# RWKV-7 time mixing by a timetable: two pairs of heads side by side, keys projected ahead

## The chip, the cores and the metric

The kernel runs on one core of one Trainium2 chip. The metric is the device time of one execution in microseconds (us), the median of several runs. The core's engines run side by side, each taking its own instructions in a fixed order: TensorE (PE, with its weight loads shown as PEld), VectorE (DVE), ScalarE (ACT), GpSimd (POOL) and SyncE (SP), which issues nearly all transfers from HBM. Engines wait for one another through semaphores. [...]

## The reference

Two layers over 256 tokens of width 2048. Layer A is RWKV-7 time mixing and a squared-ReLU MLP, layer B chunked attention on shared keys and values and another such MLP. Each sub-layer has an RMS norm in front with shift and scale from `c`, and a gate behind. The change is in the time mixing:

```python
xr, xw, xk, xv, xa, xg = [h + xx * mu[j] for j in range(6)]
r = xr @ w_r;  k = xk @ w_k;  v = xv @ w_v
w_log = -jax.nn.softplus(-(w0 + jnp.tanh(xw @ w1) @ w2)) - 0.5
a = jax.nn.sigmoid(a0 + (xa @ a1) @ a2)
g = jax.nn.sigmoid(xg @ g1) @ g2
kk = heads(k * k_k);  kk = kk / max(|kk|, 1e-12);  k = k * (1 + (a - 1) * k_a)
def step(S, inp):                      # one token, per head
    sa = einsum('bhvk,bhk->bhv', S, -kk_t)
    S = S * w_t + sa (kk_t * a_t) + v_t k_t
    y = einsum('bhvk,bhk->bhv', S, r_t)
y = group_norm(y) * ln_w + ln_b + sum(r * k * r_k) * v
return (y * g) @ w_o
```

There are 32 heads of 64. Instead of 256 steps the kernel takes four chunks of 64 tokens, with a triangular matrix inverted per chunk and head.

## The kernel before, in words

Activations lie with features on the 128 partitions and the 256 tokens along the row, so two heads, called a pair, fill the partitions, and there are 16 pairs. Every large product is done in two halves: a weight block of 128x1024 f32 is loaded into a `raw` tile (`raw`, line 350; 6 tiles), ACT casts it to the rounded half `wH` (L360), DVE makes the rest `wL` (L363), and per 128 input features `proj2` (L394, L395) issues one 512-column matmul with `wH` and one 256-column matmul with `wL`. Such a couple is called a dense unit below: a whole 2048-wide output block of 128 features is 16 units.

The program's stages in time: the norm, the token-shifted mixtures and the values (0 to 221 us); time mixing (221 to 764 us); the output projection `out_proj`; the MLP of layer A in four quarters, each with 16 up and 16 down blocks; shared keys and values, attention, its output projection; the second MLP.

Time mixing is written as generators per pair (`class Pair`): a projection of `k` and `r` (`proj_steps`, 32 dense units), `early` (decay, gates, normalisation: ACT and DVE on 128x256 tiles), `invert` (the triangular inverse by five doubling levels, each of them PE, ACT, PE, DVE; line 103 is the 32x32 matmul) and `late` (four chunks one after the other, each of three short dependent steps, then the group norm). In each period of 16 slots one pair is in each of the four stages, so a pair takes four periods and there are 19 periods; in the last three the first products of `out_proj` (`out_steps`) take the place of the dense part. The order on each engine is set by the tile framework's planner when the program is built, with `tc.issue_after` holding dense units and small steps of a slot in turn. Sums over a head (`head_sums`, L120) are two 256-column matmuls on the halves `sH` and `sL`, the second of which POOL makes (L115).

Beside all this runs `ada`: the shifts, scales and gates are 384 steps after the first stage, each a 128x1024 load into the same `raw` tiles and one DVE multiply-add into `acc` (L421, L423). `ada()` takes one step where the code calls it: 6 per period of time mixing, one per block of `out_proj`, four per three blocks of an MLP. `ada_need` runs all steps still missing for the parts that are named.

Of the kernel before, what the change touches and what calls it, by code (L numbers as in the profile page):

```python
# [32 lines left out]
        "w0", "a0", "k_k", "k_a", "r_k", "ln_w", "ln_b"]  # L33
# [3 lines left out]
def _constants():  # L37
# [23 lines left out]
    p = np.arange(P)  # L61
    bones = (p[:, None] // C == p[None, :] // C).astype(np.float32)
    put("bones", bones)
# [10 lines left out]
class Pair:  # L74
# [3 lines left out]
    EARLY = 8  # L78

    def __init__(self, body, j, v, tw, ta, tg, e01):  # L80
        self.b, self.j, self.v, self.tw, self.ta, self.tg, self.e01 = body, j, v, tw, ta, tg, e01
        self.heads = (slice(0, C), slice(C, P))

    def s(self, name="s", bufs=10):
        return self.b.pw.tile([P, T], F32, tag=name, bufs=bufs, name=name)

    def big(self, name, bufs):
        return self.b.pw.tile([P, 4, P], F32, tag=name, bufs=bufs, name=name)

    @staticmethod  # L90
    def ch(t):
        return t.rearrange("p (c t) -> p c t", t=C)

    def each(self, o, lhsT, rhs):
        for c in range(4):
            for K in self.heads:
                self.b.nc.tensor.matmul(o(c)[K], lhsT(c)[K], rhs(c)[K], start=True, stop=True)  # L97

    def tiles(self, o, lhsT, rhs, pairs):

        for c in range(4):
            for R, K in pairs:
                self.b.nc.tensor.matmul(o[QS[K], c, :], lhsT[QS[R], c, :], rhs[QS[R], c, :], start=True, stop=True,  # L103
                                        tile_position=(H * R, H * K))

    def parts(self, func, src, scale=1.0):

        nc, pw = self.b.nc, self.b.pw
        H, L = (pw.tile([P, T], F32R, tag=n, bufs=2, name=n) for n in ("sH", "sL"))
        nc.scalar.activation(H, src, func, scale=scale)  # L110
        if func != AF.Copy:
            t = self.s("pt", 2)
            nc.scalar.activation(t, src, func, scale=scale)
            src = t
        nc.gpsimd.tensor_tensor(out=L, in0=src, in1=H, op=ALU.subtract)  # L115
        return H, L

    def head_sums(self, ps, parts):
        for i, t in enumerate(parts):
            self.b.nc.tensor.matmul(ps, self.b.bones, t, start=(i == 0), stop=(i == 1))  # L120

    def early(self):
        b, nc, j, k, r, v, s, ch = self.b, self.b.nc, self.j, self.k, self.r, self.v, self.s, self.ch
        pw, vec, cst, e01 = b.pw, b.vec, b.cst, self.e01
        lw = pw.tile([96, 2, P], F32, tag="lw", bufs=2, name="lw")
        nc.sync.dma_start(out=lw, in_=b.d["lora2"][j, :96, 0:2])
        self.lg = pw.tile([P, 2, P], F32, tag="lg", bufs=2, name="lg")
        nc.sync.dma_start(out=self.lg, in_=b.d["lora2"][j, :, 2:4])
        z = b.psm()
        nc.tensor.matmul(z[:, 0:T], lw[:, 0, :], self.tw, start=True, stop=True)  # L130
        nc.tensor.matmul(z[:, T:2 * T], lw[:, 1, :], self.ta, start=True, stop=True)

        sw, a = s(), s()
        for o, at, b0 in ((sw, 0, "w0"), (a, T, "a0")):
            nc.vector.tensor_scalar(out=o, in0=z[:, at:at + T], scalar1=vec(b0, j), scalar2=-80.0,
                                    op0=ALU.add, op1=ALU.max)
            nc.scalar.activation(o, o, AF.Exp, scale=-1.0)
# [55 lines left out]
    def invert(self):  # L193
# [23 lines left out]
        for i, K in enumerate(QS):  # L217
            n = H * (i % 2)
            nc.scalar.copy(da[K], pg[K, :, n:n + H])
            if i % 2 == 0:  # L220
                nc.scalar.mul(co[K], pg[K, :, H:C], -1.0)
# [869 lines left out]
```

## Time and profile before

| what | us |
|---|---|
| median of 3 runs | 2779.97 |
| runs, lowest to highest | 2776.5 to 2784.27 |
| profiled execution | 2773.6 |
| its span, first to last instruction | 2771.8 |
| busy time of PE, of the span | 2653.9 (96%) |
| busy time of DVE | 2087.3 (75%) |
| busy time of ACT | 1260.9 (45%) |
| busy time of POOL | 301.8 (11%) |

Busy time of PE counts each matmul from its start to a modelled end; small matmuls overlap in it. So the distance from one start to the next says more on PE than the share. The transfers moved 662.60 MB, 239 GB/s on average. The stages differ much: time mixing has its transfers at half load, the first MLP at nine tenths.

### The profile page before, as it was taken

The page shows a single profiled execution, that of the slowest core. Times are in us where ns is not written, and L with a number is a line of the kernel's source. Part 1 is how long each engine was busy: PE and PEld are TensorE (multiplying, and loading weights), DVE is VectorE, ACT ScalarE, POOL GpSimd, SP SyncE. Part 2 cuts the span into 40 slices and gives each one's busy share as a digit, 9 for nine tenths or more (in the row PEclk, how much of TensorE's full clock was granted, in tenths as well). Part 3 has the DMA queues.
Part 4 walks back from the last instruction along what each step waited for, and adds up shares of the span by engine and source line. Part 5 has one row for each costly group of instructions (what it writes and reads, how often), then busy time and mean ns, then how long its engine had stood idle before and what let it go on. Part 6 is the DMA issues. An engine that isn't in the chain of part 4 may idle for free.

```text
span 2771.8 us, 57644 instructions
## 1 busy us (share of the span) xinstructions
PE 2653.9 (96%) x23402; PEld 2217.6 (80%) x23402; DVE 2087.3 (75%) x3098; ACT 1260.9 (45%) x2214; POOL 301.8 (11%) x416
## 2 busy tenths in 40 slices
PE   6998999999998999999999899999989999999997
PEld 3677777777887888888888788877878888888886
DVE  4568778878889888888788896799786566665665
ACT  2345555556344434344344354465444344443444
POOL 0003443443220000000000200000100000000002
PEclk9999999999999999999999999999999999999999
DMA  9886556555687888888888868888876555555553
GB/s 297 269 281 193 169 171 196 176 176 162 216 302 243 298 308 305 300 314 296 299 306 302 304 218 282 268 293 268 279 242 216 187 186 186 187 183 189 185 188 122
DMA packets 217387, 662.60 MB, mean 239 GB/s; under 512 B 21408, under 2 KB 68896, under 8 KB 217120
## 3 DMA queue, kind: packets, MB, share of 16 engines
q1 hardware_dynamic: 215056, 656.36, 71.5%
q8 instruction: 184, 3.01, 0.4%
q10 hardware_dynamic: 2064, 2.54, 0.3%
q14 instruction: 83, 0.68, 0.1%
HBM read 656.72 MB, written 2.10 MB: 238 GB/s over the span
## 4 chain that ended last, share of the span: by engine, by line
PE 76%; DVE 9%; DMA 7%; issue 4%; POOL 1%; ACT 1%; DVEq 0%; SPq 0%; ACTq 0%; POOLq 0%
PE pj L394 40%; PE pj L395 20%; DMA raw<-w_ada 5%; DVE wL L363 3%; DVE acc L423 2%; PE iv L103 2%; PE gr L97 1%; DMA raw<-w_ada_kv 1%; PE m L625 1%; DVE un L504 1%; PE o L383 1%; PE ms L97 1%; POOL sL L115 1%; PE chn L276 1%; DVE aHL L506 1%
## 5 line engine op out<-in xcount | busy, mean ns | idle before, releaser
L394 PE MATMUL pj<-aHL,wH 128*128 128x512 f32 x3712 | 1353.5, 405 | 26.0 <-DVE aHL L506 22.4
L360 ACT CAST wH<-raw 128x1024 fp32r<-128x1024 f32 x772 | 807.0, 1047 | 949.4 <-PE pj L394 622.1
L363 DVE TENSOR_TENSOR wL<-raw,wH 128x1024 fp32r<-128x1024 f32 x772 | 946.1, 1228 | 290.7 <-ACT wH L360 288.8
L395 PE MATMUL pj<-aHL,wL 128*128 128x256 f32 x3712 | 1049.3, 283 | 7.5 <-DVE wL L363 7.2
L394 PEld LDWEIGHTS pj<-aHL,wH 128*128 128x128 f32 x3712 | 700.3, 189 | 199.2 <-issue 28.0
L394 PE MATMUL pj<-hHL,wH 128*128 128x512 f32 x2048 | 722.0, 397 | 4.5 <-DVE hHL L882 4.5
L395 PEld LDWEIGHTS pj<-aHL,wL 128*128 128x128 f32 x3712 | 705.3, 190 | 14.6 <-DVE wL L363 11.9
L395 PE MATMUL pj<-hHL,wL 128*128 128x256 f32 x2048 | 574.3, 281 | 4.6 <-DVE wL L363 4.5
L423 DVE SCALAR_TENSOR_TENSOR acc<-raw,ct,acc 128x1024 f32<-128x1024 f32 x360 | 470.4, 1307 | 139.8 <-DMA raw<-w_ada 104.0
L394 PEld LDWEIGHTS pj<-hHL,wH 128*128 128x128 f32 x2048 | 384.3, 188 | 97.9 <-DVE hHL L882 6.7
L395 PEld LDWEIGHTS pj<-hHL,wL 128*128 128x128 f32 x2048 | 386.8, 189 | 8.1 <-DVE wL L363 7.7
L482 POOL TENSOR_TENSOR ss<-ss,sq 128x256 f32<-128x256 f32 x56 | 65.0, 1160 | 1599.7 <-ACT sq L481 1599.4
L901 DVE SCALAR_TENSOR_TENSOR x<-pj,mod,x 128x256 f32<-128x256 f32 x256 | 123.1, 481 | 51.7 <-PE pj L395 48.8
L881 ACT CAST hHL<-t 128x256 fp32r<-128x256 f32 x128 | 51.4, 403 | 67.6 <-DVE t L880 67.3
L625 PE MATMUL m<-rawa,crep 128*32 128x256 f32 x512 | 47.4, 449 | 17.5 <-DMA rawa<-w_ada 16.9
L481 ACT ACTIVATE sq<-x 128x256 f32<-128x256 f32 x60 | 25.0, 418 | 70.5 <-DVE x L901 39.6
L880 DVE SCALAR_TENSOR_TENSOR t<-t 128x256 f32<-128x256 f32 x128 | 53.9, 422 | 3.0
L882 DVE TENSOR_TENSOR hHL<-t,hHL 128x256 fp32r<-128x256 f32 x128 | 53.4, 418 | 0.6 <-ACT hHL L881 0.5
L862 DVE TENSOR_TENSOR t<-pj,t 128x256 f32<-128x256 f32 x128 | 53.2, 417 | 0.0
L239 POOL TENSOR_TENSOR al<-da,csts 128x128 f32<-128x128 f32 x64 | 40.7, 647 | 67.4 <-PE iv L103 62.7
L861 ACT COPY t<-pj 128x256 f32<-128x256 f32 x128 | 46.6, 366 | 0.0
L685 PE MATMUL t<-aHL,wH 128*128 128x256 f32 x128 | 38.1, 298 | 5.8 <-DVE v L693 3.6
(230 smaller groups left out, 2483.0 us busy)
## 6 DMA issues: line engine op xcount, KB each, us to landing
raw<-w_ada SPq DMA_DIRECT2D x320, 512.0 KB, 4.7
raw<-w_up SPq DMA_DIRECT2D x256, 512.0 KB, 4.9
raw<-w_down SPq DMA_DIRECT2D x256, 512.0 KB, 4.3
rawa<-w_ada SPq DMA_DIRECT2D x64, 512.0 KB, 6.8
raw<-w_ada_kv SPq DMA_DIRECT2D x64, 512.0 KB, 5.4
raw<-w_k SPq DMA_DIRECT2D x32, 512.0 KB, 4.2
raw<-w_r SPq DMA_DIRECT2D x32, 512.0 KB, 4.7
raw<-w_o SPq DMA_DIRECT2D x32, 512.0 KB, 5.2
```

Source lines behind the costliest of these rows:

```text
L97: self.b.nc.tensor.matmul(o(c)[K], lhsT(c)[K], rhs(c)[K], start=True, stop=True)
L103: self.b.nc.tensor.matmul(o[QS[K], c, :], lhsT[QS[R], c, :], rhs[QS[R], c, :], start=True, stop=True, tile_position=(H * R, H * K))
L360: nc.scalar.copy(Hf, raw)
L363: eng.tensor_tensor(out=Lf, in0=raw, in1=Hf, op=ALU.subtract)
L394: nc.tensor.matmul(ps, H[:, i, :], a(kt), start=(kt == 0), stop=False)
L395: ins = nc.tensor.matmul(ps[:, 0, :], L[:, i, :], a(kt)[:, 0, :], start=False, stop=(kt == KT - 1))
L423: nc.vector.scalar_tensor_tensor(out=acc, in0=raw, scalar=ck, in1=acc, op0=ALU.mult, op1=ALU.add)
L482: (eng or nc.gpsimd).tensor_tensor(out=self.ss, in0=self.ss, in1=sq, op=ALU.add)
L625: nc.tensor.matmul(ps[g:g + 32, part, :W], crep[:, kt, :], raw[:, i, :], start=(part == 1 and kt < 4), stop=(part == 0 and kt >= KT - 4), ...
L880: nc.vector.scalar_tensor_tensor(out=t, in0=t, scalar=0.0, in1=t, op0=ALU.max, op1=ALU.mult)
L882: nc.vector.tensor_tensor(out=h[:, 1, :], in0=t, in1=h[:, 0, :], op=ALU.subtract)
L901: nc.vector.scalar_tensor_tensor(out=x, in0=ps[:, i, :], scalar=self.mods[(layer, 5)][:, n:n + 1], in1=x, op0=ALU.mult, op1=ALU.add)
```

## The change

`class Quad` takes the place of `class Pair`: two pairs stand side by side in one tile, 512 elements wide, so that nearly each DVE, ACT and POOL instruction of the stage does twice the work and there are half as many. Each step is entered in a timetable by slot and rank (`at(slot, rank)`); a quad takes 46 slots (0 to 45, and a load 8 slots ahead), a new one starts every 20 slots, there are 8, so 186 slots in all. In a slot the steps of up to three quads are written by rank, then the dense units of a fixed table (`UNITS`, 32 in 20 slots), then casts of coming weight halves (`HALVES`), then one `ada` step in six of the 20 slots. While the timetable runs, PE, DVE, ACT and POOL issue in the order in which it is written (`STRICT`, `InOrder`); the planner keeps the rest of the program.

The 16 blocks of `k` are projected ahead of the timetable in one stretch of 256 dense units with 23 `ada` steps; the 16 units of `r` per pair stay in the slots, those of the first quad ahead of them.

Other edits: head sums are f32 matmuls of 512 columns per head, with no halves. `w0` and `a0` come in as a 97th row of the low-rank matmul. The wide matrices of two quads lie in the former buffer of `xk` (`hold`). There are 3 `ms` banks and no `gr` bank; the 128-column matmuls into `gr` become twice as many of 64 columns. `raw` has 4 tiles, and 4 more (2 in the attention) from a second pool after time mixing. Of the output projection 72 unit-sized pieces (128 features of one block, three 256-column matmuls) stand in the timetable, before 88 in the last three periods. `ada` steps up to the end of the timetable: 77, before 102; the parts (0, 4) and (0, 3) are asked for after `out_proj` and not ahead of it.

On PE, in the middle of time mixing, before (`pj` is a dense unit, `iv` the inverse, `chn` and `py` the chunk steps of another pair):

```order
L304 MATMUL py<-ar,sa 64x64 x2
L103 MATMUL iv<-tt,al 32x32 x16
L394 MATMUL pj<-aHL,wH 128x512
L395 MATMUL pj<-aHL,wL 128x256
L394 MATMUL pj<-aHL,wH 128x512
L395 MATMUL pj<-aHL,wL 128x256
L276 MATMUL chn<-bk,mk 64x64 x2
L279 MATMUL chn<-zs,kr 64x64 x2
L103 MATMUL iv<-u,xs 32x32 x16
```

And after, at slots 17 to 20 of a quad (all of the timetable carries line 79; `ms` is a sum, a transpose or a product with a bank of its own):

```order
L79 MATMUL py<-hold,sa 64x64 x4
L79 MATMUL ms<-hold,kh 64x64 x16
L79 MATMUL iv<-u,xs 32x32 x32
L79 MATMUL ms<-hold,kh 64x64 x16
L79 MATMUL iv<-tt,al 32x32 x32
L79 MATMUL ms<-sl,csts 64x512 x2
L79 MATMUL iv<-u,xs 32x32 x32
L79 MATMUL iv<-tt,al 32x32 x32
L79 MATMUL ms<-tw,lw 128x256 x2
```

Two dense units stood between the two halves of a level; now other small products do, in groups twice as large. Counted over one period, PE changes between 128-, 64- and 32-wide tiles some 40 times per pair before, and 28 times per two pairs now.

On SP, where the first key blocks are loaded (at the start of time mixing), before:

```order
L350 DMA raw<-w_k 128x1024 x2
L350 DMA raw<-w_r 128x1024 x2
L350 DMA raw<-w_k 128x1024 x2
L350 DMA raw<-w_r 128x1024 x2
L350 DMA raw<-w_k 128x1024
L126 DMA lw<-lora 96x256
```

and after:

```order
L542 DMA raw<-w_k 128x1024 x4
L542 DMA raw<-w_ada 128x1024
L542 DMA raw<-w_k 128x1024
L542 DMA raw<-w_ada 128x1024
L542 DMA raw<-w_k 128x1024
L178 DMA lw<-lora 97x512
```

Key blocks and `ada` blocks now follow each other without the small work between.

On DVE, at the end of the first up blocks of the first MLP, where the gate (0, 5) is asked for (`t` and `hHL` close an up block, `mod_5` is the gate), before:

```order
L862 TENSOR_TENSOR t<-pj,t 128x256
L880 SCALAR_TENSOR_TENSOR t<-t 128x256
L363 TENSOR_TENSOR wL<-raw,wH 128x1024
L882 TENSOR_TENSOR hHL<-t,hHL 128x256
L363 TENSOR_TENSOR wL<-raw,wH 128x1024
```

and after:

```order
L615 SCALAR_TENSOR_TENSOR acc<-raw,ct,acc 128x1024
L1108 TENSOR_TENSOR hHL<-t,hHL 128x256
L615 SCALAR_TENSOR_TENSOR acc<-raw,ct,acc 128x1024 x3
L555 TENSOR_TENSOR wL<-raw,wH 128x1024
L615 SCALAR_TENSOR_TENSOR acc<-raw,ct,acc 128x1024
L555 TENSOR_TENSOR wL<-raw,wH 128x1024
L631 TENSOR_TENSOR mod_5_75<-m,bada 128x8
```

Ahead of the first down weights (the two `wL` rows) now stand the `ada` steps that `ada_need` still misses.

The core of the diff:

```diff
+class Quad:
+    PERIOD = 20
+    LAST = 45
+    def at(self, slot, rank):
+        def add(f):
+            self.steps.setdefault(slot, []).append((rank, f))
+        return add
...
+    def head_sums(self, t):
+        ps = self.b.psm()
+        for K in self.heads:
+            self.b.mm(ps[K], self.b.cst("ones")[K, 0:C], t[K], start=True, stop=True)
+        return ps
...
+        def first(l):
+            def f():
+                xs = self.xs = self.half("xs")
+                if l < 5:
+                    pi = product(self.al, self.tt, own)
+                    act.copy(xs, pi)
+                    if l < 4:
+                        level(l + 1)
...
+        def second(l):
+            def f():
+                if l < 5:
+                    pi = product(self.xs, self.ui, own)
+                    dve.tensor_tensor(out=self.ui, in0=self.ui, in1=pi, op=ALU.add)
+                    turn()
...
+        for l in range(1, 6):
+            at(14 + 2 * l, 2)(first(l))
+            at(15 + 2 * l, 2)(second(l))
...
 class Body:
-    RAW_BUFS = 6
     W_BUFS = 3
-    DRAIN_STEPS = (14, 14, 16)
-    ADA_SLOTS = (1, 3, 6, 9, 11, 14)
+    UNITS = (0, 0, 0, 0, 5, 5, 0, 4, 3, 4, 3, 0, 0, 0, 0, 5, 3, 0, 0, 0)
+    HALVES, LAST_HALVES = (6, 7, 13, 16), (7, 10, 13, 16)
+    ADA_SLOTS = (0, 2, 12, 15, 18, 19)
...
+    def raw_tile(self):
+        self.nraw += 1
+        if self.more and self.nraw % (self.more[1] + 4) >= 4:
+            return self.more[0].tile([P, HK * P], F32, tag="raw", bufs=self.more[1], name="raw")
+        return self.wp.tile([P, HK * P], F32, tag="raw", bufs=4, name="raw")
...
-            self.ada_need((0, 2), (0, 4), (0, 3))
-            self.out_proj(self.pp, "w_o", self.y_hl, (0, 2), self.o_ps)
+            self.ada_need((0, 2))
+            with self.more_raw(4):
+                self.out_proj(self.pp, "w_o", self.y_hl, (0, 2), self.o_ps)
+            self.ada_need((0, 4), (0, 3))
...
+            for n, _ in enumerate(dense(range(KT), xk, lambda i: k[:, i, :])):
+                if n % HK == 0:
+                    half()
+                if n % 11 == 10:
+                    self.ada()
...
+            nc.strict = self.STRICT
+            quads = [Quad(self, q, k, v, tw, ta, tg, hold[:, q % 2, :]) for q in range(NQ_)]
...
+            for slot in range(-8, end - Quad.PERIOD + Quad.LAST + 1):
+                while steps and steps[0][0] == slot:
+                    steps.pop(0)[3]()
...
+                for _ in range(self.UNITS[at] if p < NQ_ else 2 * (at > 5)):
+                    next(big, None)
+                for _ in range((self.HALVES if p < NQ_ else self.LAST_HALVES).count(at)):
+                    half()
...
+                if at in self.ADA_SLOTS:
+                    self.ada()
```

More of the change, by code (lines that the diff above doesn't have):

```diff
@@ L106, in parts @@
[L106 to L120, printed above, removed]
@@ L538, in run @@
         self.ada_done = set()
+        self.nraw, self.more = 0, None
         self.adas = self.ada_all()
@@ L828, in layer_a @@
+            for _ in big:
+                pass
             self.fin(HK)
+            nc.strict = ()
         return v
```

682 lines of the change are left out of this document (395 added, 287 removed).

## Prediction

> **What bounds the kernel now.** First the page's busy shares and the chain of waits, then the table of stages.
>
> ```profile
> span 2771.8 us, 57644 instructions
> PE 2653.9 (96%) x23402; PEld 2217.6 (80%) x23402; DVE 2087.3 (75%) x3098; ACT 1260.9 (45%) x2214; POOL 301.8 (11%) x416
> PE 76%; DVE 9%; DMA 7%; issue 4%; POOL 1%; ACT 1%; DVEq 0%; SPq 0%; ACTq 0%; POOLq 0%
> ```
>
> PE carries three quarters of the chain. The windows (us, busy time and instructions by engine, granted clock, DMA share, GB/s) are the middle of time mixing, its last periods, `out_proj`, the MLP's start and rest, and attention's `out_proj` with what is around it:
>
> ```profile
> 310.00:684.00 374.00, 367.25 (x7023) 284.82 (x7022) 298.86 (x564) 203.42 (x567) 155.49 (x204) 0.99 0.54 172
> 684.00:764.00 80.00, 78.44 (x1414) 66.45 (x1413) 64.85 (x108) 33.76 (x92) 18.23 (x27) 1.00 0.68 220
> 764.00:841.00 77.00, 62.61 (x418) 54.63 (x418) 63.71 (x73) 30.54 (x43) 17.44 (x14) 0.90 0.88 299
> 841.00:1000.00 159.00, 155.21 (x993) 134.40 (x993) 135.91 (x184) 72.43 (x101) 0.00 (x0) 0.99 0.82 279
> 1000.00:1530.00 530.00, 523.51 (x3450) 454.22 (x3450) 446.50 (x550) 225.20 (x285) 4.76 (x4) 1.00 0.89 303
> 1930.00:2030.00 100.00, 90.28 (x562) 77.39 (x561) 81.55 (x106) 43.09 (x59) 14.69 (x14) 0.95 0.81 268
> ```
>
> In time mixing PE is busy 367 of 374 us, DVE 299, and transfers take half their time: PE is the bound, and only fewer or cheaper PE starts shorten the stage. In the MLP PE, DVE and DMA are all close to full. The line that multiplies the low-rank weights runs twice a pair and gives the period; PE's timeline shows what its time is spent on:
>
> ```profile
> L130 PEld LDWEIGHTS ms<-tw,lw x26: 186/188/189, 310.4 to 683.4; 96*128 96x128 f32 x26
> 242.10 0.40 PE L394 MATMUL pj<-aHL,wH 128*128 128x512 f32 x1
> 242.34 0.28 PE L395 MATMUL pj<-aHL,wL 128*128 128x256 f32 x1
> 242.55 0.68 PE L97 MATMUL ms<-csts,v 64*64 64x64 f32 x16
> 243.16 0.50 PE L394 MATMUL pj<-aHL,wH 128*128 128x512 f32 x1
> 243.50 0.28 PE L395 MATMUL pj<-aHL,wL 128*128 128x256 f32 x1
> 243.62 0.40 PE L394 MATMUL pj<-aHL,wH 128*128 128x512 f32 x1
> 243.85 0.28 PE L395 MATMUL pj<-aHL,wL 128*128 128x256 f32 x1
> 243.97 0.40 PE L394 MATMUL pj<-aHL,wH 128*128 128x512 f32 x1
> ```
>
> 26 records are 13 pairs, so 12 periods lie from 310.4 to 683.4: 31.1 us a pair, 62.2 for two. Undisturbed, a dense unit goes from 243.62 to 243.97: 0.35. Around a group of 64-wide matmuls it costs more: 0.21 from 242.34 to 242.55 where 0.12 follows otherwise (243.50 to 243.62), and 0.34 instead of 0.23 behind it. A change of tile size is thus worth some 0.10.
>
> **The change, part by part.** *One period P of a quad against 62.2.* PE loses the 32 units of `k`: 32 x 0.35 = 11.2. It loses mode changes: 40 per pair, 80 for two, against 28 in the new order: 52 x 0.10 = 5.2 (bounds 0 and 8, as the groups' neighbours may already overlap or the pause be longer). The head sums lose POOL's half:
>
> ```profile
> PE py L120 <- POOL sL L115: 7.7, 4, 2.2
> L120 PE MATMUL ms<-sH,bones 128*128 128x256 f32 x24 | 8.3, 348 | 0.0
> L318 PE MATMUL py<-tg,lg 128*128 128x256 f32 x48 | 13.1, 385 | 0.0
> ```
>
> That wait is 7.7 us in the 384 us from 300 to 684, 12.3 pairs: 0.6 a pair, 1.2 for two. For it come sums in plain f32 over 512 columns on 64 partitions, which no row shows. There are three sums a quad (of squares, of the bonus, of the group norm), each of one matmul per head. By the nearest row of that type, L318, 256 columns take 0.385, 512 then 0.77; three sums are 2.3 if the two heads, on separate halves of the array, run beside each other, less the twelve rounded ones of two pairs at the 0.12 of the timeline, 1.4: +0.9. One after the other they make +3.2. Nothing below +0.9 is likely, since f32 is the slower type in these rows. I take +1.3, near the first, since the 64-wide groups of the timeline (16 in 0.68) overlap too. So P = 62.2 - 11.2 - 5.2 - 1.2 + 1.3 = 45.9. The small matmuls themselves keep their number of columns and are counted unchanged.
>
> The new thing is strict order: PE now stands at whatever waits. What is queued behind it are the other two quads' small products and the dense units of the slot. The price is a hop from PE to ACT and back:
>
> ```profile
> 261.87 0.45 PE L103 MATMUL iv<-tt,al 32*32 32x32 f32 x32 [0.25 <-DVE tt L235]
> 262.39 0.27 ACT L241 COPY xs<-iv 128x128 f32<-128x128 f32 x1
> 262.71 0.45 PE L103 MATMUL iv<-u,xs 32*32 32x32 f32 x32 [0.39 <-ACT xs L241]
> ```
>
> Where nothing stands between the halves of a level PE is idle 0.39. The added wait is between 0 and 20 slots x 0.39 = 7.8 per period. I take 0: one step a slot means the partner engine has some 2.3 us (45.9 / 20) for 0.3 to 0.7 us of work, and the measured 62.2 holds such waits already.
>
> DVE must fit under P, in the new order's instructions per quad, by the rows of 310 to 684:
>
> ```profile
> L423 DVE SCALAR_TENSOR_TENSOR acc<-raw,ct,acc 128x1024 f32<-128x1024 f32 x65 | 86.3, 1328 | 0.1
> L363 DVE TENSOR_TENSOR wL<-raw,wH 128x1024 fp32r<-128x1024 f32 x47 | 62.1, 1321 | 11.1 <-ACT wH L360 11.0
> L261 DVE TENSOR_TENSOR mk<-gr,csts 128x512 f32<-128x512 f32 x12 | 8.3, 688 | 1.7 <-PE gr L97 1.0
> L135 DVE TENSOR_SCALAR s<-ms,vecs 128x256 f32<-128x256 f32 x24 | 10.6, 478 | 4.2 <-PE ms L131 4.0
> L148 DVE TENSOR_TENSOR_SCAN s<-csts,s 128x256 f32<-128x256 f32 x12 | 8.6, 718 | 1.5 <-ACT s L142 1.5
> L300 DVE SCALAR_TENSOR_TENSOR zs<-zs,pc,chn 128x64 f32<-128x64 f32 x24 | 6.6, 273 | 5.9 <-PE chn L295 5.9
> ```
>
> Six `acc` and four `wL` at 1.325 are 13.3, fifteen of 512 at 0.69 10.3, twenty of 256 at 0.48 9.6, two scans 1.4, the small rest 3: 37.6, below 45.9. DVE doesn't bound unless PE falls below it. ACT's casts and copies, 203 us for 12 pairs, are 34 for two, and less in the new form.
>
> *The keys in front.* 256 units x 0.35 = 90 of PE. Besides, 32 key and 23 `ada` loads pass through four tiles:
>
> ```profile
> raw<-w_k SPq DMA_DIRECT2D x32, 512.0 KB, 4.2
> raw<-w_ada SPq DMA_DIRECT2D x320, 512.0 KB, 4.7
> L360 ACT CAST wH<-raw 128x1024 fp32r<-128x1024 f32 x49 | 51.3, 1046 | 42.1 <-PE pj L394 40.9 <-DMA raw<-w_r 0.8
> SPq L350 <- DVE wL L363: 29.7, 9, 7.3
> ```
>
> 55 loads of 0.524 MB at the 303 GB/s of the MLP's row take 95; a tile is held for 4.7 + 1.05 + 1.32, about 7 us, so four tiles hand out one each 1.75 us, 55 in 96; DVE needs 55 x 1.325 = 73. Three resources within 6 us of each other: I take 97, bounds 92 and 110. On SP's queue the key loads move ahead of all `w_r` loads, with `ada` loads between; what stands behind them is the first `w_r` and `lw`, needed only after the stretch, so their delay costs the first dense units of `r` at most one landing, 4.7. The `r` units of quad 0 alone add 32 x 0.35 = 11. The timetable then has two filling periods (32 without late steps, then 45: 77), six full ones, 6 x 45.9 = 275, and 26 draining slots holding `out_proj` pieces: 38 (30 to 50, since 80 us took 80 of PE for 88 pieces and the last steps before). Time mixing: 97 + 11 + 77 + 275 + 38 = 498 where it took 764 - 221 = 543: -45.
>
> *What it pushes back.* 16 pieces fewer of `out_proj` stand in mixing, +5.6 (16 x 0.35; the third matmul of a piece may make it 8). The 25 `ada` steps missing (77 for 102) come back: of the MLP's norm, 4 run ahead in a row, 4 x 1.33 = +5 (0 to 8). At the gate (0, 5), 11 run between the up and the down blocks: DVE 14.6, transfers 11 x 0.524 / 303 = 19, cover the 5.6 us of units already cast: I take 14.6 - 5.6 = +9 (0 to 19). Ahead of attention's `out_proj`, 11 instead of one: +5, less, since its window has PE idle 10 us already (0 to 14). Queued behind each burst on DVE are the `wL` that PE waits for, on SP the weight loads. The value stage before has only four tiles for six: SP there already waits 29.7 us, in 9 waits; +2 (0 to 10). Eight tiles in the MLP cover late loads: PE idles 10.3 in 841 to 1530 (159 + 530 less 155.21 + 523.51), -4 (0 to -8). Sum: 5.6 + 5 + 9 + 5 + 2 - 4 = +23. The 97th row, the new buffer and the 64-column grams (as many columns) I cost at nothing, under PE's other work.
>
> Net -45 + 23 = -22 on the profiled execution's 2773.6 (span 2771.8 and 1.8 around it): 2751.6. The median, 2780.0, stands 6.4 above that execution: 2758.
>
> **The rivals.** *Faster still.* A mode change costs 0.14 and not 0.10 (mine comes from one place): 52 x 0.04 = 2.1 more, P = 43.8, -13 over six periods; and the +14 of the first two bursts finds cover because eight tiles hold their loads, with 6 less elsewhere in the +23: 2758 - 33 = 2725. For it: DVE would still fit (37.6), and POOL's 155.49 in 12 pairs is 26 a quad. Against: the MLP's DMA share of 0.89 leaves the bursts' loads little room.
>
> *A wash.* Four tiles starve the key stretch at the upper bound (110, +13), and the bursts cost 9 more: 2780. For it: three resources level at 95. Against: the MLP keeps PE at 524 of 530 with the same three.
>
> *Slower: strict order shows a hop in every slot.* P = 45.9 + 7.8 = 53.7; six full periods +47, two filling slots' worth +2: 2758 + 49 = 2807. It decides from P = 49.6 on (22 us more over six periods), and reads as slower by 0.3% from P = 50.9. For it: the row with 0.39 idle, with 32 of them dense units gone that used to fill such holes. Against: three quads in each slot, and 32 units still there.
>
> One more, a clock that falls in the fill and drain, where dense units are few:
>
> ```profile
> 821.00:845.00 24.00, 13.64 (x65) 11.16 (x64) 21.31 (x34) 8.44 (x15) 1.41 (x2) 0.73 0.76 255
> ```
>
> Where PE works 13.6 of 24 us the granted clock is 0.73, in 764 to 841 0.90, in 684 to 764, which is full, 1.00. If fill and drain (115 us) were granted 0.9, that is +12: 2770, on this side of no change. [...]
>
> **How the numbers follow.** Forecast 0.38 with the clock's case in it (some 0.05), faster still 0.22, wash 0.16, slower 0.24. The forecast's own range is 2735 to 2771, from the bounds of the bursts (-19, +13). The range over all: the faster case's 2725 less half its step, 2712, to the slower's 2807, rounded to 2805. What a measurement of this kernel can tell from no change is about 0.3%, 8.3 us (its three runs reach from 2776.5 to 2784.27). Faster by more than that: 0.38 + 0.22 = 0.60; within it 0.16; slower 0.24.
>
> **What would show it.** P from two firsts of `lw` products: 46, or 54 for the slower rival; PE's waits in the timetable put down to ACT `xs` or DVE `tt` and `u`, under 1 us a period or near 8. The key stretch at 97, with SP waiting for `wL`. Time mixing 498 long in all. PE idle some 9 us behind the last up block of the MLP's first quarter, with 11 `acc` in a row on DVE. The forecast is wrong if DVE's sum or a chain through three engines sets P and not PE, which would show as PE busy far below 45 in 46.

## The result and the profile after

The changed kernel takes 2857.24 us (median of four runs, 2852.83 to 2863.45) against 2778.23 beside it on the same chips: a ratio of 1.028, 95% interval 1.026 to 1.031. The prediction said 2758. The profiled execution takes 2857.3 against 2773.6 before; the comparisons below are between these two.

The page of the changed kernel, its busy times and the granted clock in 40 slices (the span is 2855.5 us):

```profile
PE 2654.1 (93%) x23882; PEld 2225.8 (78%) x23882; DVE 2058.9 (72%) x2893; ACT 1194.1 (42%) x1845; POOL 214.8 (8%) x296
PEclk9999989899999999999999999999989999999999
```

PE is busy as long as before, 2654 us, though the forecast counted work away from it. What is longer is the time in which PE is not busy, and part of what counts as busy is slow: the clock is below nine tenths in two slices of time mixing and in one ahead of the second MLP.

The windows of time mixing (us, busy time and instructions by engine, then granted clock, DMA share, GB/s): the key stretch, the first quad's first period alone, six periods, and the drain:

```profile
221.00:328.00 107.00, 98.29 (x575) 83.50 (x576) 72.21 (x86) 40.40 (x61) 0.99 (x2) 0.94 0.78 256
342.00:382.00 40.00, 28.84 (x610) 23.29 (x612) 29.03 (x39) 14.80 (x26) 13.62 (x15) 0.92 0.49 151
382.00:696.00 314.00, 269.53 (x6919) 212.92 (x6907) 198.07 (x323) 121.79 (x243) 88.43 (x114) 0.93 0.37 113
745.00:790.00 45.00, 39.34 (x731) 33.44 (x720) 28.61 (x46) 13.82 (x31) 1.90 (x4) 0.89 0.49 154
```

In the six periods PE is busy 270 of 314 us where it was busy 367 of 374, and no engine has taken its place: DVE has 198. So the stage has no engine as its bound any more. By the period, PE is busy 44.9 us and idle 7.4; before, for two pairs, it was busy 61.2 and idle 1.1. The rows of the `tw` product give the period. An f32 matmul leaves two records in these traces, so a quad has four, and for seven quads first to last is six periods and the last quad's four products:

```profile
L79 PE MATMUL ms<-tw,lw x28: 378/634/796, 382.4 to 695.9; 97*128 97x256 f32 x28
```

(695.9 - 382.4) / 6 = 52.2 us, which is how the period is given for every run below; the forecast had 45.9. The first of the six still belongs to the fill, with two quads; the five full ones, from 435.3 to 694.4, take 51.8 each. The one-ring run below has the same time mixing and shows 52.7, so differences of half a microsecond say nothing. Half of these matmuls take 634 ns or more where the shortest takes 378: those of four quads, and in the 2 us from their starts (382.4, 435.4, 537.0 and 694.4) the granted clock is 0.50, while it is 1.00 at the other three. They stand just behind the inverse's groups and so make the clock look worse than it is; over the six periods it is 0.93. Period by period (windows from one quad's first `tw` to the next one's), the two with a clock of 0.99 take 51.0 each, the two with 0.89 and 0.85 take 52.9 and 55.1. So even at nearly full clock the period is 5 us above the forecast.

What PE waits for in the six periods, with the total, the times and the longest in us:

```profile
PE chn L79 <- DVE zs L79: 15.8, 12, 2.2
PE iv L79 <- issue: 11.8, 12, 3.0
PE iv L79 <- DVE tt L79: 9.9, 10, 1.1
PE iv L79 <- ACT xs L79: 2.4, 5, 0.5
```

These are three different costs. The first is a place in an order. DVE's timeline around one such wait:

```profile
572.99 1.49 DVE L79 SCALAR_TENSOR_TENSOR acc<-raw,ct,acc 128x1024 f32<-128x1024 f32 x1
575.57 1.57 DVE L79 TENSOR_TENSOR wL<-raw,wH 128x1024 fp32r<-128x1024 f32 x1 [1.09 <-ACT wH L79]
577.07 0.46 DVE L79 SCALAR_TENSOR_TENSOR zs<-zs,pc,chn 128x64 f32<-128x64 f32 x2
```

The state `zs`, 0.46 us of work for which PE stands, is queued behind an `ada` step and a weight remainder, and that remainder itself waits 1.09 us for ACT's cast. The third and fourth rows are the hops between the halves of an inverse level. The second, "issue", was 0.4 us in all in the middle of time mixing before:

```profile
PE iv L103 <- issue: 0.4, 1, 0.4
```

PE's timeline shows where it falls now, and the windows what follows:

```profile
528.04 0.52 PE L79 MATMUL iv<-u,xs 32*32 32x32 f32 x37 [0.84 <-issue]
528.49 1.15 PE L79 MATMUL ms<-hold,kh 64*64 64x64 f32 x32
529.69 0.69 PE L79 MATMUL iv<-tt,al 32*32 32x32 f32 x59
531.63 0.25 PE L79 MATMUL iv<-tt,al 32*32 32x32 f32 x5 [1.25 <-issue]
531.82 1.08 PE L79 MATMUL ms<-sl,csts 64*64 64x512 f32 x4
532.82 0.75 PE L79 MATMUL iv<-u,xs 32*32 32x32 f32 x64
534.66 0.66 PE L79 MATMUL iv<-tt,al 32*32 32x32 f32 x54 [1.09 <-DVE tt L79]
536.70 0.37 PE L79 MATMUL iv<-tt,al 32*32 32x32 f32 x10 [1.38 <-issue]
```

```profile
530.00:535.00 5.00, 2.66 (x158) 1.62 (x146) 2.91 (x5) 1.69 (x3) 0.64 (x1) 1.00 0.53 190
535.00:540.00 5.00, 3.62 (x115) 2.56 (x100) 1.57 (x3) 0.54 (x2) 0.00 (x0) 0.59 0.32 110
540.00:545.00 5.00, 5.00 (x88) 2.54 (x84) 3.25 (x6) 2.51 (x5) 0.00 (x0) 0.50 0.23 51
```

PE stops in the middle of a group, with nothing to wait for that the profile shows. Between two such stops lie 37 + 32 + 59 = 128 matmuls, then 5 + 4 + 64 + 54 = 127 (a record may be missing), each with its weight load (the page counts 23882 of both). The trace shows what PE may be waiting for: its own code. The instruction queue, q8, moved 187 packets of 16 KB (3.06 MB) in this run, one for 255 of PE's 2 x 23882 records, about what lies between two stops; and each of the 14 stops of the six periods ends 1.2 to 1.6 us after such a packet has landed. That is a reading of the trace; no run tries it by itself. Three of the stops in 9 us cost 0.84, 1.25 and 1.38. Some 60 small matmuls go by in 0.7 us, and no dense unit stands between the groups. PE is busy 2.66 of 5 us, and then the granted clock falls: 0.59 from 535 to 540, 0.50 from 540 to 550, 0.75 from 550 to 556. The drop comes with several scattered pauses, none of them longer than 1.38 us.

Added up over windows of 4 us, (1 - granted clock) x time is 48 us from 222 to 804, where it was 7 from 222 to 780 in the kernel before. Of the 48, 22 lie in the six periods. That is the most it can have cost: at a clock of 0.50 a `tw` product took 634 ns for 378, the first of its four 796 for 483, so less than twice as long, and the time is lost only where PE sets the pace.

Behind time mixing, the last matmuls of `out_proj`, the first and last down matmuls of both MLPs, and the transposes in the stage of shared values. First the kernel before, then the changed one:

```profile
L384 PE MATMUL o<-aHL,wH x128: 276/283/469, 684.4 to 780.4; 128*128 128x256 f32 x128
L394 PE MATMUL pj<-hHL,wH x1024: 387/391/504, 933.9 to 1582.4; 128*128 128x512 f32 x171
L943 PE MATMUL m<-csts,vf x32: 270/271/272, 1702.4 to 1790.3; 128*128 128x128 f32 x32
L394 PE MATMUL pj<-hHL,wH x1024: 387/398/500, 2122.3 to 2755.9; 128*128 128x512 f32 x171
```

```profile
L576 PE MATMUL o<-aHL,wH x24: 278/284/416, 789.3 to 803.4; 128*128 128x256 f32 x24
L586 PE MATMUL pj<-hHL,wH x1024: 387/396/796, 973.9 to 1631.9; 128*128 128x512 f32 x171
L1169 PE MATMUL m<-csts,vf x32: 269/272/333, 1756.4 to 1856.2; 128*128 128x128 f32 x32
L586 PE MATMUL pj<-hHL,wH x1024: 386/397/505, 2209.6 to 2840.0; 128*128 128x512 f32 x171
```

The lag is 23.0 us at the end of the `o` products, 40.0 at the first down block (+17: the norm, the gate and two output blocks, see below), 49.5 at the end of that MLP (+9.5), 65.9 at the end of the shared values (+16), 87.3 at the second MLP's first down block (+21) and 84.1 at its end. So of 84 us only 23 arise up to the last `o` product, and 61 come later. But that product doesn't close the same work in both kernels: 96 pieces (six blocks) now stand in this form, 128 (eight blocks) before, and the other two blocks follow as dense units. The first such matmuls, from the last `o` product to the first down block, before and after:

```profile
L394 PE MATMUL pj<-aHL,wH 128*128 128x512 f32 x384 | 137.2, 401 | 6.7 <-DVE aHL L506 6.7
L586 PE MATMUL pj<-aHL,wH 128*128 128x512 f32 x416 | 147.8, 400 | 5.9 <-DVE aHL L694 5.8
```

These 32 units are 11.2 us at 0.35, so about 34 of the 84 belong to time mixing with its output projection and 50 to code that was hardly touched. From the last `o` product to the second MLP's first down block PE is idle 77 us where it was idle 50, and (1 - granted clock) x time is 48 us where it was 21. So late work and, behind it, a lowered clock go on there too: at the gate PE stands 6.9 us in one piece for ACT's `wH`, and in the 7 us behind that the clock is 0.50.

### The profile page after: what moved, and what is told of

Its sections match the earlier page's. It is cut to its first block, busy times and chain, and to the rows that moved or that the text cites. A ratio compares the mean times of both kernels' runs of the same rounds, so it can differ in the third digit from the quotient of the medians.

```text
span 2855.5 us, 57632 instructions
## 1 busy us (share of the span) xinstructions
PE 2654.1 (93%) x23882; PEld 2225.8 (78%) x23882; DVE 2058.9 (72%) x2893; ACT 1194.1 (42%) x1845; POOL 214.8 (8%) x296
## 3 DMA queue, kind: packets, MB, share of 16 engines
q8 instruction: 187, 3.06, 0.4%
## 5 line engine op out<-in xcount | busy, mean ns | idle before, releaser
L552 ACT CAST wH<-raw 128x1024 fp32r<-128x1024 f32 x732 | 765.3, 1046 | 994.9 <-PE pj L586 585.9
L587 PE MATMUL pj<-aHL,wL 128*128 128x256 f32 x3488 | 990.5, 284 | 9.2 <-DVE wL L555 9.0
L586 PEld LDWEIGHTS pj<-aHL,wH 128*128 128x128 f32 x3488 | 664.3, 191 | 198.6 <-issue 22.2
L587 PEld LDWEIGHTS pj<-aHL,wL 128*128 128x128 f32 x3488 | 668.8, 192 | 16.8 <-DVE wL L555 16.0
L1127 DVE SCALAR_TENSOR_TENSOR x<-pj,mod,x 128x256 f32<-128x256 f32 x256 | 123.5, 482 | 55.7 <-PE pj L587 51.9
L1107 ACT CAST hHL<-t 128x256 fp32r<-128x256 f32 x128 | 51.5, 403 | 70.0 <-DVE t L1106 69.8
L79 PE MATMUL pj<-aHL,wL 128*128 128x256 f32 x256 | 73.2, 286 | 2.0 <-DVE wL L79 1.7
L79 PEld LDWEIGHTS pj<-aHL,wH 128*128 128x128 f32 x256 | 49.0, 191 | 13.8 <-DVE a L79 0.8
```

Of the source, the lines that this page charges most:

```text
L79: return (lambda *args, **kw: self.tc.keep_in_program_order(f(*args, **kw))) if callable(f) else f
L552: nc.scalar.copy(Hf, raw)
L586: nc.tensor.matmul(ps, H[:, i, :], a(kt), start=(kt == 0), stop=False)
L587: ins = nc.tensor.matmul(ps[:, 0, :], L[:, i, :], a(kt)[:, 0, :], start=False, stop=(kt == KT - 1))
L1107: nc.scalar.copy(h[:, 0, :], t)
L1127: nc.vector.scalar_tensor_tensor(out=x, in0=ps[:, i, :], scalar=self.mods[(layer, 5)][:, n:n + 1], in1=x, op0=ALU.mult, op1=ALU.add)
```

## The experiments

All are the changed kernel with one edit, but for two that edit the kernel before; times are medians, ratios against the kernel before on the same chip. The changed kernel's own interval is 1.026 to 1.031, and a run whose interval lies much within it can't be told from it by the whole time. Waits and busy times are those of the one profiled execution.

**The planner in place of strict order.**

```diff
-    STRICT = ("tensor", "vector", "scalar", "gpsimd")
+    STRICT = ()
```

> The planner orders the timetable's instructions on PE, DVE, ACT and POOL; nothing else is changed. Theory (strict order makes PE stand: 14.2 us for zs, 7.7 for tt, some 11 of issue pauses between 435 and 694 us, and the low clock that follows): the period falls from 51.8 to about 46, and the time to some 2815. Rival (the timetable is short of dense work wherever the small products stand, whoever orders it): period 50 to 54, time 2845 to 2870.

The `tw` products of its six periods:

```profile
L520 PE MATMUL ms<-tw,lw x28: 379/379/483, 380.9 to 698.0; 97*128 97x256 f32 x28
```

2858.11 us, 1.031 (1.028 to 1.033), period 52.9. Strict order is not what costs: the planner's order of the same instructions has the same period, and PE is idle 33 of 317 us there.

**The dense units spread over the slots.**

```diff
-    UNITS = (0, 0, 0, 0, 5, 5, 0, 4, 3, 4, 3, 0, 0, 0, 0, 5, 3, 0, 0, 0)
-    HALVES, LAST_HALVES = (6, 7, 13, 16), (7, 10, 13, 16)
+    UNITS = (2, 1, 2, 2, 1) * 4
+    HALVES, LAST_HALVES = (2, 7, 12, 17), (7, 10, 13, 16)
```

> The same 32 dense units of a period, spread as (2, 1, 2, 2, 1) four times over the slots, with the halves' slots moved along. Theory (cover: small products without dense work between them drain the instruction pages, show every hop and let the clock fall): PE's pauses mostly close, clock above 0.98 in the timetable, period 46 to 47, time about 2817. Rival (the slot's own chain through ACT and DVE is what is long): period 51 to 52, time 2850 to 2865.

The `tw` products of its six periods, and their window:

```profile
L79 PE MATMUL ms<-tw,lw x28: 379/379/795, 383.4 to 681.3; 97*128 97x256 f32 x28
```

```profile
383.00:681.00 298.00, 274.04 (x6915) 211.68 (x6906) 204.97 (x323) 121.36 (x241) 86.52 (x114) 0.97 0.38 117
```

2849.62 us, 1.027 (1.025 to 1.029), period 49.6, clock 0.97. That is half of what the theory wanted in the period, and the whole time can't be told from the changed kernel's. PE's wait for `zs` is gone from its list of waits, while the stops without a semaphore stay (16.0 us in all, 13.7 before this edit); PE is idle 4.0 us a period. The `o` products end at 791.4, 12 us sooner, but some 10 of that are lost again behind.

**The keys back in the timetable.** Before the timetable only the first quad's keys; 64 units a period.

```diff
+    UNITS64, HALVES64 = (3, 3, 3, 3, 4) * 4, (1, 4, 6, 9, 11, 14, 16, 19)
-    ADA_SLOTS = (0, 2, 12, 15, 18, 19)
+    ADA_SLOTS = (0, 2, 5, 10, 12, 15, 17, 18)
...
+            def kr_steps(q):
+                yield from dense((2 * q, 2 * q + 1), xr, lambda i: k[:, i, :])
+                yield from r_steps(q)
...
```

> The keys' 32 units of a quad stand in the timetable again (64 units a period, spread 3, 3, 3, 3, 4), only the first quad's are in front; ada steps 8 a period instead of 6 and none in the front stretch (74 in all, 77 before). The keys are computed from the mixture of r, which leaves out the use of xk, not any work. Theory (cover): period 46 + 11 = 57, time mixing 64 shorter, time about 2793. Rival (chain of the slot, to which dense units add): period 63, mixing 18 shorter, time about 2839.

The `tw` products of its six periods, and their window:

```profile
L79 PE MATMUL ms<-tw,lw x28: 379/379/484, 299.1 to 648.5; 97*128 97x256 f32 x28
```

```profile
299.00:648.00 349.00, 332.43 (x7285) 263.11 (x7274) 250.17 (x371) 143.68 (x275) 97.51 (x114) 0.99 0.49 155
```

2830.62 us, 1.020 (1.018 to 1.022). The period is 58.2, that is 47.0 besides 11.2 for the keys' units; PE is busy 332 of 349 us and the clock 0.99. With twice the dense units the pauses have cover: PE is idle 2.8 us a period. The products of `o` end at 768.8, 35 us sooner than in the changed kernel and 12 sooner than in the kernel before. The 12 are about the 11.2 of the two blocks that come later, so up to there quads with the keys in their slots are level with pairs, with 28 `ada` steps fewer done; that they beat pairs is not shown. The run still ends 59 us behind the kernel before by its span, so here nearly all of the loss lies behind time mixing. (The keys can't simply go back: `hold` lies in the buffer of `xk`, which is why this run takes them from the mixture of `r`.)

**Nine `ada` steps a period.**

```diff
-    ADA_SLOTS = (0, 2, 12, 15, 18, 19)
+    ADA_SLOTS = (0, 2, 4, 8, 12, 14, 15, 18, 19)
```

> Nine ada steps a period instead of six (slots 4, 8 and 14 added), so that about 102 are done by the end of the timetable, as in the kernel before. Theory (the lag of 25 steps is what costs 60 us behind time mixing): the norm, the gate, the shared keys and values and the stage behind attention give back 25 to 40 us, time mixing costs 0 to 8 more, time about 2825. Rival (the two rings of raw tiles, not the lag, are the cost there): 2850 to 2865.

The `tw` products of its six periods:

```profile
L79 PE MATMUL ms<-tw,lw x28: 493/634/795, 389.7 to 724.2; 97*128 97x256 f32 x28
```

2887.36 us, 1.041 (1.038 to 1.044), 30 us worse. Period 55.7: three steps, 4.0 us on an engine that is idle a third of the time, cost 3.5. The shortest `tw` product is now at 493 ns, where in the changed kernel those at a clock of 1.00 took 378 to 485, so all quads after the first seem to start at a lowered clock; just behind the first four of these starts it is 0.50 to 0.60 (390 to 394, 446 to 450, 502 to 506 and 558 to 562 us). The `o` products end 41.5 us later than in the changed kernel, and behind them only 11 of the 61 us come back. By stage it is less simple: from the shared values to the second MLP the lag grows by 5.0 and not by 21.4, but in the first MLP by 22.7 and not by 9.5, where PE waits 23 us for `wL`. So the lag in `ada` steps is the likely cause of the 21 in that stretch, and not of most of the whole loss.

**Useless work behind each inverse product.**

```diff
-            pi = pp.tile([P, 16, H], F32, tag="iv", bufs=1, name="iv")[:, 0:8, :]
+            iv = pp.tile([P, 16, H], F32, tag="iv", bufs=1, name="iv")
+            pi = iv[:, 0:8, :]
             self.tiles(pi, lhsT, rhs, pairs)
+            b.mm(iv[:, 8:16, :], b.cst("ident"), b.csts[:, 0:256], start=True, stop=True)
```

> Adds one useless f32 matmul (128x128 by 256 columns, about 0.43 us of full array) behind each of the ten inverse products of a quad, into the unused half of their bank: 8 x 10 x 0.43 = 34 us more work on PE. Theory (the low clock, some 48 us lost between 222 and 804 us against 7 in the kernel before, follows stretches where the array does little): the clock stays up, at least 25 of those 48 come back, most of the added work fits into PE's pauses, and the time falls to 2825 to 2845. Rival (the clock is a by-product, PE only waits): the work adds to the chain, 2865 to 2890.

The `tw` products of its six periods, and their window:

```profile
L79 PE MATMUL ms<-tw,lw x28: 376/379/634, 384.4 to 706.9; 97*128 97x256 f32 x28
```

```profile
384.00:707.00 323.00, 289.30 (x7006) 228.17 (x7006) 198.07 (x324) 121.79 (x243) 89.71 (x114) 0.97 0.36 110
```

2883.64 us, 1.039 (1.036 to 1.041): the rival's number. The period rose from 52.2 to 53.7, by 1.5 for 4.3 us of work. The clock did rise, from 0.93 to 0.97, which is at most 2 us a period, and the stops without a semaphore fell from 13.7 to 5.5 us in six periods, as work between the groups would have it. But the work costs more than both save.

**The kernel before with two rings of raw tiles,** four and two in turn, as the changed kernel has them in the attention.

```diff
+    def raw_tile(self):
+        self.nraw = getattr(self, "nraw", 0) + 1
+        if self.nraw % 6 >= 4:
+            return self.wp.tile([P, HK * P], F32, tag="raw2", bufs=2, name="raw")
+        return self.wp.tile([P, HK * P], F32, tag="raw", bufs=4, name="raw")
```

> The kernel before with its six raw tiles split into a ring of four and a ring of two, taken in turn (four, then two), nothing else. Theory (the split lets key and value loads overtake the ada loads, so that ada loads come in pairs and the weights behind them late): the stages behind time mixing lose 30 to 50 us, 2806 to 2826. Rival (a ring is a ring): 2772 to 2782.

SP's timeline in the stage of shared values, of the kernel before and of this one:

```profile
1727.17 0.33 SPq L350 DMA_DIRECT2D raw<-w_ada  x1
1728.31 1.75 SPq L350 DMA_DIRECT2D raw<-w_v_shared  x2
```

```profile
1754.40 1.79 SPq L356 DMA_DIRECT2D raw<-w_ada  x2
1758.87 7.13 SPq L356 DMA_DIRECT2D raw<-w_v_shared  x4
```

Its down matmuls of the second MLP:

```profile
L400 PE MATMUL pj<-hHL,wH x1024: 387/398/500, 2148.0 to 2781.7; 128*128 128x512 f32 x171
```

2797.19 us, 1.007 (1.005 to 1.009), between the two expectations and nearer to the theory's 2806. The `o` products end 8 us sooner than before, and the second MLP begins 26 us later: 34 lost between, 20 of it up to the end of the first MLP and 14 from the shared keys on. With two rings the planner lets loads go in another order: two `ada`, then four of the weights, and the changed kernel has the same pairs in that stage.

**The kernel before with fewer `ada` steps in time mixing.**

```diff
-                    if slot in self.ADA_SLOTS and p >= 2:
+                    if slot in self.ADA_SLOTS and p >= 6:
```

> The kernel before with its ada steps in time mixing begun four periods later: 78 instead of 102, nothing else. Theory (bursts of missing steps ahead of the norm, the gate and the second output projection): time mixing unchanged, 10 to 20 us more behind it, 2786 to 2796. Rival (the bursts are hidden): 2772 to 2782.

Its `o` matmuls:

```profile
L384 PE MATMUL o<-aHL,wH x128: 277/283/468, 671.1 to 798.0; 128*128 128x256 f32 x128
```

2794.06 us, 1.007 (1.005 to 1.009), as the theory had it, though at another place: here all missing steps run ahead of `out_proj`, whose last products come 18 us later, after a mixing that ended 10 sooner. The price of 24 missing steps is 14 us by the profiled spans (2785.8 against 2771.8) and 20 by the medians.

**One ring of six in `out_proj` and the MLPs** instead of four and four.

```diff
-        if self.more and self.nraw % (self.more[1] + 4) >= 4:
+        if self.more and (self.more[1] == 6 or self.nraw % (self.more[1] + 4) >= 4):
...
-            with self.more_raw(4):
+            with self.more_raw(6):
...
```

> The changed kernel with one ring of six tiles in both output projections of layer A's time mixing and both MLPs, in place of four and four; the attention keeps four and two. Theory (the split rings cost the stages): the norm and the first MLP give back 10 to 20 us, 2837 to 2847. Rival (eight tiles are worth more than the order of loads): 2855 to 2870.

2887.19 us, 1.040 (1.038 to 1.042), 30 us worse, outside both expectations. The run changes two things, one ring for two and six tiles for eight, so it doesn't say what the ring's form alone is worth. The four lasting tiles are idle in these stages, and the new ones exist only from a stage's start; that the loss is a prefetch across the stages' borders is argued, not shown.

**28 of 32 units left out of each period.**

```diff
-            def dense(todo, hl, dst):
+            def dense(todo, hl, dst, work=True):
...
-                        self.proj2(ps, {kt // HK: w}, lambda kt: hl[:, kt, :, 0:T], (kt, kt + 1))
+                        if work or kt in (0, KT - 1):
+                            self.proj2(ps, {kt // HK: w}, lambda kt: hl[:, kt, :, 0:T], (kt, kt + 1))
...
-                return dense(range(2), xr, lambda i: r[:, i * T:(i + 1) * T])
+                return dense(range(2), xr, lambda i: r[:, i * T:(i + 1) * T], q == 0)
```

> 28 of the 32 dense units of each period are left out (the projection of r keeps its first and last unit per block, so r is not r); the loads, casts, remainders and the closing copy of each block stay. 28 x 0.35 = 9.8 us of PE work go. Theory (with only 32 units the period is the chain of small steps through PE, ACT and DVE, not PE's work): the period falls by less than half of that, 51.8 to 47 or more. Rival (PE's work sets the period): 51.8 - 9.8 = 42.

The `tw` products of its six periods, and their window:

```profile
L79 PE MATMUL ms<-tw,lw x28: 379/630/795, 381.0 to 679.8; 97*128 97x256 f32 x28
```

```profile
381.00:680.00 299.00, 227.19 (x6551) 178.83 (x6548) 203.23 (x323) 121.19 (x243) 91.58 (x114) 0.84 0.39 118
```

One run, 2846.05 us; the period is 49.8. Of 9.8 us of PE work taken away 2.4 show. The clock falls to 0.84: 8.0 us a period at most, where it was 3.7 (0.07 x 314 / 6). So PE's busy time falls by 7.0 a period (from 44.9 to 37.9) and not by 9.8, and its idle time rises by 4.6 (from 7.4 to 12.0). More of the work turned into waiting than came off the period, and the rest, 2.8, fits the lower clock: PE's work alone doesn't set this period.

**No `ada` step in the key stretch nor in the timetable** (the call in the stretch and all `ADA_SLOTS` removed).

> No ada step in the key stretch nor in the timetable (77 steps move behind them, so the whole time says nothing; the two stages are read). Theory (in strict order an ada step of 1.33 us on DVE stands ahead of a small step, as three more cost 3.8 a period): six fewer give 45 to 47 a period. Key stretch without the 23 ada loads: PE's 256 units, 90 to 94, where it took 107. Rival (DVE's place in the order costs nothing below its throughput): period 50 to 52, and stretch 105 if the casts and not the loads hold it.

ACT's wait for key loads, in the changed kernel's stretch (221 to 328) and in this one's (221 to 311), then this one's window of the stretch and its `tw` products:

```profile
ACT wH L552 <- DMA raw<-w_k: 48.3, 20, 6.0
```

```profile
ACT wH L552 <- DMA raw<-w_k: 7.7, 2, 7.5
```

```profile
221.00:311.00 90.00, 87.63 (x491) 76.01 (x492) 47.45 (x63) 40.66 (x62) 0.99 (x2) 0.98 0.58 187
```

```profile
L79 PE MATMUL ms<-tw,lw x28: 379/379/795, 365.7 to 663.6; 97*128 97x256 f32 x28
```

The stretch takes 90 us, PE's 256 units, with PE busy 87.6. So the 23 `ada` steps cost 16 to 17 there, and the wait for key loads falls from 48.3 to 7.7. The period is 49.6: six steps fewer, 8 us of DVE, give 2.6, less than expected. The stops without a semaphore fall to 4.5 us, so they may hang on the load traffic too (DMA share 0.17 for 0.37); no run takes the two apart.

**A clear path for `zs`.**

```diff
-    HALVES, LAST_HALVES = (6, 7, 13, 16), (7, 10, 13, 16)
-    ADA_SLOTS = (0, 2, 12, 15, 18, 19)
+    HALVES, LAST_HALVES = (6, 8, 14, 16), (7, 10, 13, 16)
+    ADA_SLOTS = (0, 2, 11, 15, 18, 19)
```

> The weight halves of slots 7 and 13 move to 8 and 14, and the ada step of slot 12 to 11, so that no remainder wL and no ada step stands on DVE between the chunk product of slot 14 and its state zs. Theory: PE's wait for zs (14.2 us from 435 to 694, some 2.8 a period) falls below 1 a period and the time by 12 to 18, 2840 to 2846. Rival (the wait turns up at another step of the slot): 2850 to 2865.

The longest of PE's waits in its six periods (total, times, longest), and its `tw` products:

```profile
PE iv L79 <- issue: 11.6, 11, 2.7
PE iv L79 <- DVE tt L79: 10.7, 11, 1.1
```

```profile
L79 PE MATMUL ms<-tw,lw x28: 379/634/795, 379.0 to 688.3; 97*128 97x256 f32 x28
```

2841.62 us, 1.024 (1.021 to 1.026), 16 us better than the changed kernel by the medians and 13 by the ratios, whose intervals just overlap; 12 to 18 was expected. The wait for `zs`, the largest before, is gone from the list. But the period fell only from 52.2 to 51.5, and the clock in the six periods from 0.93 to 0.89; the rest of the gain lies in the fill and the drain, and some 3 us ahead of the stage, which the edit can't have caused: the first `tw` product stands between 337.5 and 343.7 in the runs that change nothing ahead of it.

**Both, spread and clear.** `UNITS` as in the spread run, halves in slots 2, 8, 14 and 17, `ada` as in the last.

> The spread of the dense units and the clear path for zs together: units (2, 1, 2, 2, 1) four times over, halves in slots 2, 8, 14 and 17, the ada step of slot 12 in 11. Theory (the lost cover and the state behind wL are two separate costs of the timetable): the period falls from 51.8 to 47 to 49, the time to 2822 to 2836; what follows time mixing stays 60 to 70 us longer than before, so it doesn't reach the kernel before. Rival (what one gives, the low clock or the other takes back): period 50 to 52, 2840 to 2852.

The `tw` products of its six periods:

```profile
L79 PE MATMUL ms<-tw,lw x28: 379/379/795, 379.2 to 683.1; 97*128 97x256 f32 x28
```

2849.54 us, 1.029 (1.024 to 1.033): the rival. Period 50.6, between those of the two edits alone. The waits say why nothing was added: the spread alone had already taken away the wait for `zs`, so the clear path had nothing left to clear. What remains in PE's list is mostly stops without a semaphore (14.9 us in all) and the hops (8.1).

No run reached the kernel before.

## Why the prediction was wrong

The forecast for the profiled execution was 2751.6, the measured 2857.3: 106 us. By its own terms, 69 of them lie in time mixing (221.6 to 788, 566 long, forecast 498): 9 in the key stretch, 3 in the first quad's `r`, 17 in the fill, 35 in the six full periods and 5 in the drain. And 37 lie behind it (60 more than before, forecast 23).

- **"I take 0" for the added wait of a period.** This is the step that failed. The forecast counted PE's work and took it for the period. P is 52.2, not 45.9. PE's busy time fell from 61.2 to 44.9, by 16.3, which is the forecast's step from 62.2 to 45.9; its idle time rose from 1.1 to 7.4, by 6.3, which is the whole miss. That the work came out so exactly is partly luck: in the periods at a clock of 0.99 PE is busy only 42.1 and 42.8, and the low clock elsewhere made up the rest. The 7.4 are the wait for `zs` (2.6), stops without a semaphore (2.3), the hops to `tt` and `xs` (2.1) and small ones. With 64 units a period the timetable runs at 47.0 plus the keys' 11.2 and PE is idle 2.8; with 32 units the work alone no longer sets the pace (28 more away: 2.4 of 9.8 us). The argument for 0, that the measured 62.2 held such waits already, overlooked two things: it held only 1.1 of them, and half of the dense work that covered them was moved out by the same change.
- **The slower rival** named that direction and nearly that period (53.7), with a chance of 0.24, but for the wrong reason: not a hop in each slot because of strict order, since the planner's order gives 52.9, and the hops are 2.1 of its 7.8 a period. And its sum ended at 2807, because it kept the other terms.
- **The clock** stood in the forecast as +12 us at fill and drain, with a chance of some 0.05. Low stretches occur in the full periods too (0.93 over all), up to 48 us in the stage. The trace of before had the sign of it, 0.73 where PE worked 13.6 of 24 us.
- **The keys in front:** forecast 97, measured 107, inside its bounds, and by the sign that was given: SP waits 39 us in 24 waits for `wL` to free a tile. Without `ada` it is PE's 90.
- **Fill:** 77 forecast, 93.5 measured (341.8 to 435.3). The first period has one quad and 32 units, and lasts 40 us with PE busy 29: a slot takes about 2 us even with one quad in it. The second, with two quads, lasts 52.9, as long as a full one.
- **Behind time mixing:** of the 17 from the last `o` product to the first down block, 11.2 are the 32 units of two output blocks. The 6 that remain for the norm and the gate are fewer than the 14 (5 + 9) forecast; the stop at the gate is 6.9. The stretch with the burst ahead of the second output projection (5) lost 21. The gain of eight tiles (-4) was a loss of 9.5, though PE waits a little less in that MLP (9.2 us, before 10.4): what grew is the time at a lowered clock (8 us by the sum above, before none). The shared keys and values, counted at nothing, lost 16; the +2 ahead of time mixing came to nothing (its first product starts at 221.6, before at 221.7). The two rings explain part: in the kernel before, they cost 14 from the shared keys on. The lag explains 11 (nine steps a period) to 20 (the kernel before). If costs from different kernels may be added, which no run shows, 16 to 25 of the 61 stay without a proven cause; eight tiles as one ring were not tried.

## What to carry to other kernels

Where an engine is the bound only because long work covers the waits of short work, don't subtract the long work at its own price: look at what it covered, and expect those waits to show. In this kernel a microsecond of dense work taken from a period gave 0.54 to 0.77 (from 64 units to the changed kernel's 32, or to the same 32 spread evenly) and then 0.25 (32 to 4). An engine's busy share below its old level, with none risen to take its place, is the sign. Before two savings are added, see in the waits of each run whether they remove the same wait. And a buffer pool split in two, or bursts of work moved out of a stage, show their price in stages that the diff doesn't touch, so time every stage, not only the edited one.

## What the runs showed of the hardware

Groups of 64 records of 32x32 matmuls (32 matmuls in the program) pass in 0.75 us, and PE stops with no semaphore to wait for, 14 times in the six periods of the changed kernel (12 of them at such a group), for 0.25 to 2.96 us; in the stretch shown the stops are 128 and 127 records apart; in the kernel before, with dense units between groups half as large, such waits were 0.4 us in 344. That they are code loading is a reading of the traces. The instruction queue q8 moved 187 packets in the changed kernel and 184 in the kernel before, one for 255 and 254 of PE's records (2 x 23882 and 2 x 23402). And all 15 stops in the middle of time mixing of the two (14 and 1) end 1.2 to 1.6 us after a packet of that queue has landed. With useless work between the groups the stops took 2.3 us from 435 to 694 us, where the changed kernel has 11.2; without `ada` steps, and so with fewer loads, 4.3 us from 400 to 640, where it has 9.9. Why a packet comes late was not tried by itself. And with pauses of 0.84, 1.25, 1.09 and 1.38 us within 9.5 us (527.2 to 536.7), and PE busy 6.2 of the 10 us from 528 to 538, the granted clock went down to 0.50 and stayed there from 540 to 550; what sets such a drop off was not tried by itself either.
